# A 90-degree rotation of an 8192 x 8192 matrix: the first block of columns taken as 256, 256 and 512 rows and the last as 512 and 512, all loads in 16 KB rows, two of the last outputs in load buffers

## The chip, the cores and the metric

One core of a Trainium2 chip runs the kernel. The metric is the device time of one execution in microseconds (us). The kernel before takes 1276.25 us (median of three runs, 1274.88 to 1278.71). The limit for calling a kernel faster or slower is 2%.

## The reference

```python
x = np.random.randn(8192, 8192).astype(np.float32)   # 268 MB in, 268 MB out
def reference(x, k):        # k = 1
    return np.rot90(x, k)
```

Output row `8191 - c` is input column `c`. Nothing is computed: every element is read once and written once.

## The kernel before

The matrix is taken in blocks of 1024 rows by 4096 columns. A block is eight loads of 128 rows (2 MB each, 16 KB a row). VectorE copies each load into eight tiles `ar` of 512 columns, reversing the order of the columns inside each group of 128; TensorE transposes 128 x 128 pieces into PSUM, the memory that it writes to; ScalarE evicts (copies) PSUM into an output tile `ot` of 16 KB a partition (two evictions), and issues its transfer. A block has eight outputs of 2 MB.

```python
    a_pool = ctx.enter_context(tc.tile_pool(name="a_pool", bufs=2))   # loads
    r_pool = ctx.enter_context(tc.tile_pool(name="r_pool", bufs=68))
    o_pool = ctx.enter_context(tc.tile_pool(name="o_pool", bufs=2))   # outputs
    ...
def macro_tiles(N, M):
    for r0 in range(0, N, R):                     # R = 1024
        widths = [W] * (M // W)                   # W = 4096
        ...
        if r0 + R == N:
            widths[-1:] = [2048, 1024, 1024]
        ...
    for r0, c0, C in tiles:
        q = W // C                                # row groups of one load
        for t0 in range(0, RT, q):                # RT = 8
            if loads < 2:
                a = o_pool.tile([P, W], dt, tag="o")
            else:
                a = a_pool.tile([P, W], dt, tag="a")
            loads += 1
            nc.sync.dma_start(out=a, in_=x[...])  # queue of the SyncEngine
            ...                                   # eight VectorE copies a -> ar
        for g0 in range(0, C // P, G):            # G = 4
            ot = o_pool.tile([P, W], dt, tag="o")
            ...                                   # transposes, two evictions
                    nc.scalar.dma_start(out=dst, in_=o[...])   # queue of ScalarE
```

There are two buffers for loads and two for outputs, 16 KB a partition each, beside the 68 tiles `ar` of 2 KB. The first two loads borrow the output buffers, so four loads are queued at once. And a scheduler hands buffers to tiles and orders instructions; each engine then runs its own list in that order. In the views of the profile PE is TensorE, PEld its weight loads, DVE VectorE, ACT ScalarE, POOL GpSimd and SP the SyncEngine; a q after a name stands for the engine's sequencer, which issues transfers.

## Time and profile before

| | before |
|---|---|
| time | 1276.25 us |
| moved | 537.55 MB, mean 422 GB/s |
| busy: PE, ACT, DVE | 56%, 37%, 28% |
| first output issued | 54.4 us |
| last load landed | 1246.8 us |

From the profile's page, kernel before: the span, and then the mean busy share of the 16 DMA engines in tenths and the rate in GB/s, in 40 slices of 31.9 us.

```profile
span 1274.2 us, 10388 instructions
DMA  9999999999999999999999999999999999999998
GB/s 375 366 427 427 427 428 431 429 428 428 430 428 430 428 427 429 429 429 429 427 427 427 429 427 428 427 427 429 428 427 426 424 423 429 427 425 422 420 408 338
```

The kernel is bound by its transfers, and they are not at their best in the first two slices and the last two. The Trainium skill, "HBM Reference", section Specifications (TRN2), says that a core that streams alone reaches about 425 GB/s, bounded by its 16 DMA engines; the 427 to 431 of most middle slices agree within 2%. At 428 GB/s the bytes need 1256 us, so a change of the ends alone cannot win more than about 18 us, 1.4%.

The same kernel by windows. Columns: stretch in us, its length, busy time of PE, PEld, DVE, ACT and POOL with their instructions, granted clock of TensorE, busy share of the DMA engines, GB/s.

```profile
20.00:40.00 20.00, 2.06 (x6) 0.87 (x6) 8.97 (x26) 0.00 (x0) 0.00 (x0) 1.00 0.96 362
40.00:60.00 20.00, 11.94 (x78) 10.87 (x79) 8.32 (x24) 7.37 (x4) 0.00 (x0) 1.00 0.92 366
60.00:80.00 20.00, 7.17 (x40) 6.70 (x38) 5.55 (x16) 3.67 (x3) 0.00 (x0) 0.66 1.00 415
...
1240.00:1250.00 10.00, 5.50 (x41) 5.22 (x42) 2.77 (x8) 5.72 (x4) 0.00 (x0) 0.92 0.80 337
1250.00:1260.00 10.00, 8.04 (x63) 7.53 (x62) 0.00 (x0) 6.24 (x4) 0.00 (x0) 0.91 0.87 365
1260.00:1270.00 10.00, 3.05 (x28) 2.77 (x26) 0.00 (x0) 4.66 (x3) 0.00 (x0) 0.77 0.91 383
```

From 20 to 54 us the loads run alone in two buffers, because no output can start before eight loads have landed. From 80 to 160 us the rate is 427 to 433. At the end the last load lands at 1246.8 us, and from 1240 us on the transfers that are left move 337 to 383 GB/s.

### The profile page before, as it was taken

Reading aid. Unit: us, or ns where it says so; the run is one execution under the profiler, and the core shown is the slowest. Engines: PE = TensorE matmul, PEld = TensorE weight load, DVE = VectorE, ACT = ScalarE, POOL = GpSimd, SP = SyncE. Lnnn points to the kernel's source line nnn. Section 1 sums busy time; section 2 is a strip of 40 time slices with the busy share of each in tenths; the row PEclk is TensorE's granted clock in tenths of the full one; section 3 lists DMA queues with packets and bytes.
Section 4 is the critical chain, followed back from the end, with each engine's and each line's share of the span. In section 5 each row is a group of like instructions: output and inputs, shape, how many; then the busy total and the mean of one; then the engine's idle time right before and its main releaser. Section 6 shows DMA issues by size and latency. Waiting matters only on the chain.

```text
span 1274.2 us, 10388 instructions
## 1 busy us (share of the span) xinstructions
PE 719.2 (56%) x4096; PEld 685.5 (54%) x4096; DVE 355.2 (28%) x1024; ACT 466.9 (37%) x257; POOL 0.7 (0%) x6
## 2 busy tenths in 40 slices
PE   1455556556655665556546565565565665665564
PEld 0355556555554655556546555565555554665564
DVE  4422232223222322232223222322232222321210
ACT  0233343334334333343334333433343333434444
POOL 0000000000000000000000000000000000000000
PEclk9968686877777677776886867768777778678878
DMA  9999999999999999999999999999999999999998
GB/s 375 366 427 427 427 428 431 429 428 428 430 428 430 428 427 429 429 429 429 427 427 427 429 427 428 427 427 429 428 427 426 424 423 429 427 425 422 420 408 338
DMA packets 39105, 537.55 MB, mean 422 GB/s; under 512 B 4112, under 2 KB 4112, under 8 KB 6160
## 3 DMA queue, kind: packets, MB, share of 16 engines
q1 hardware_dynamic: 20480, 268.44, 49.8%
q10 hardware_dynamic: 18576, 268.44, 49.8%
q8 instruction: 32, 0.52, 0.2%
q14 instruction: 17, 0.14, 0.0%
HBM read 268.44 MB, written 268.44 MB: 421 GB/s over the span
## 4 chain that ended last, share of the span: by engine, by line
DMA 84%; DVE 12%; issue 2%; ACT 1%; PE 0%; DVEq 0%; SPq 0%; ACTq 0%
DMA a<-in_x_dram 81%; DVE ar L111 12%; DMA out_dram<-ot 3%; ACT ot L133 1%; PE ps L128 0%; DVEq L111 0%; SPq L100 0%; ACTq L133 0%; ACTq L141 0%
## 5 line engine op out<-in xcount | busy, mean ns | idle before, releaser
L128 PE MATMUL ps<-ident,ar 128*128 128x128 f32 x4096 | 719.2, 358 | 543.8 <-ACT ot L133 500.2
L128 PEld LDWEIGHTS ps<-ident,ar 128*128 128x128 f32 x4096 | 685.5, 192 | 577.3 <-ACT ot L133 530.5
L133 ACT COPY ot<-ps 128x2048 f32<-128x2048 f32 x256 | 465.6, 1870 | 789.3 <-DMA out_dram<-ot 733.5
L111 DVE COPY ar<-a 128x512 f32<-128x512 f32 x1024 | 355.2, 421 | 894.4 <-DMA a<-in_x_dram 894.4
L133 ACT ACT_TABLE_LOAD x1 | 1.3, 1283 | 10.9 <-DVE ar L111 10.9
masks.py:199 POOL TENSOR_SCALAR_AFFINE_SELECT ident<-ident 128x128 f32<-128x128 f32 x1 | 0.3, 292 | 0.1
masks.py:197 POOL MEMSET ident<- 128x128 f32 x1 | 0.2, 204 | 0.3 <-POOLq L160 0.3
L160 POOL MEMSET const-bfloat16-1.0<- 128x1 bf16 x1 | 0.1, 102 | 0.0
L160 POOL MEMSET const-uint8-127<- 128x1 uint8 x1 | 0.1, 102 | 0.0
L160 POOL MEMSET const-float32-0.0<- 128x1 f32 x1 | 0.1, 99 | 0.2 <-issue 0.2
L160 POOL MEMSET const-float32-1.0<- 128x1 f32 x1 | 0.1, 99 | 0.0
## 6 DMA issues: line engine op xcount, KB each, us to landing
a<-in_x_dram SPq DMA_DIRECT2D x128, 2048.0 KB, 16.6
out_dram<-ot ACTq DMA_DIRECT2D x127, 2048.0 KB, 15.9
out_dram<-ot ACTq DMA_DIRECT2D x2, 1024.0 KB, 5.7
```

Of the source, the lines that this page charges most:

```text
L111: nc.vector.tensor_copy(out=ar[:], in_=a[:, u, j * CH : (j + 1) * CH].rearrange("r (b m) -> r b m", m=P)[:, :, ::-1],)
L128: nc.tensor.transpose(ps[:, PW - 1 - w, t * P : (t + 1) * P], chunks[t, g * P // CH][:, g % (CH // P), :], ident,)
L133: nc.scalar.copy(o[:, G - PW - h : G - h, :], ps[:])
L160: nc = _bacc.Bacc("TRN2", target_bir_lowering=False, num_devices=1)
```

## The change

The intent: start the first outputs earlier by a first block that is complete after two loads, keep all loads at 16 KB a row at the end as well, and let the last block's first two outputs use the load buffers that have gone idle.

```diff
-        widths = [W] * (M // W)
-        if r0 + R == N:
-            widths[-1:] = [2048, 1024, 1024]
+            rows = [RT]
+            if r0 == 0 and c0 == 0:
+                rows = [2, 2, 4]
+            if r0 + RT * P == N and c0 + W == M:
+                rows = [4, 4]
...
-            if loads < 2:
-                a = o_pool.tile([P, W], dt, tag="o")
+            if loads in (2, 3):
+                a = o_pool.tile([P, E], dt, tag="o")
...
+        R = rt * P
+        G = E // R          # E = 4096: an output tile stays 16 KB a partition
...
-            ot = o_pool.tile([P, W], dt, tag="o")
+            if last and g0 < 2 * G:
+                ot = a_pool.tile([P, E], dt, tag="a")
+            else:
+                ot = o_pool.tile([P, E], dt, tag="o")
```

Output tiles keep their size, so a block of fewer rows is written in shorter rows: 1 KB for 256 rows, 2 KB for 512, 4 KB for 1024. Note which loads take the output buffers: 2 and 3, the loads of the second block, in place of 0 and 1.

More of the change, by code (lines that the diff above doesn't have):

```diff
@@ L10 @@
 P = 128
-R = 1024
-RT = R // P
+RT = 8
 W = 4096
 CH = 512
-G = 4
-PW = 2
+E = 4096
+PB = 2048
 def whole_reads(nc):
@@ L46, in macro_tiles @@
 def macro_tiles(N, M):
-    for r0 in range(0, N, R):
-        widths = [W] * (M // W)
-        if r0 == 0:
-            widths[:1] = [4096]
-        if r0 + R == N:
-            widths[-1:] = [2048, 1024, 1024]
-        c0 = 0
-        for C in widths:
-            yield r0, c0, C
-            c0 += C
+    for r0 in range(0, N, RT * P):
+        for c0 in range(0, M, W):
+            rows = [RT]
[3 more added lines that the diff above has]
+                rows = [4, 4]
+            r = r0
+            for n in rows:
+                yield r, n, c0
+                r += n * P
 @with_exitstack
@@ L87 @@
     loads = 0
-    for r0, c0, C in tiles:
-        last = (r0, c0, C) == tiles[-1]
-        q = W // C
+    for r0, rt, c0 in tiles:
+        last = (r0, rt, c0) == tiles[-1]
+        R = rt * P
+        G = E // R
+        PW = PB // R
         chunks = {}
-        for t0 in range(0, RT, q):
-            if loads < 2:
-                a = o_pool.tile([P, W], dt, tag="o")
+        for t in range(rt):
+            if loads in (2, 3):
+                a = o_pool.tile([P, E], dt, tag="o")
             else:
@@ L98 @@
             loads += 1
-            a = a.rearrange("r (q c) -> r q c", q=q)
             nc.sync.dma_start(
-                out=a,
-                in_=x[r0 + t0 * P : r0 + (t0 + q) * P, c0 : c0 + C].rearrange(
-                    "(q r) c -> r q c", q=q
-                ),
-            )
-            for u in range(q):
-                for j in range(C // CH):
-                    ar = r_pool.tile([P, CH // P, P], dt, tag="ar")
-                    nc.vector.tensor_copy(
-                        out=ar[:],
-                        in_=a[:, u, j * CH : (j + 1) * CH].rearrange(
-                            "r (b m) -> r b m", m=P
-                        )[:, :, ::-1],
-                    )
-                    chunks[t0 + u, j] = ar
-        for g0 in range(0, C // P, G):
-            ot = o_pool.tile([P, W], dt, tag="o")
+                out=a[:], in_=x[r0 + t * P : r0 + (t + 1) * P, c0 : c0 + W]
+            )
+            for j in range(W // CH):
+                ar = r_pool.tile([P, CH // P, P], dt, tag="ar")
+                nc.vector.tensor_copy(
+                    out=ar[:],
+                    in_=a[:, j * CH : (j + 1) * CH].rearrange(
+                        "r (b m) -> r b m", m=P
+                    )[:, :, ::-1],
+                )
+                chunks[t, j] = ar
+        for g0 in range(0, W // P, G):
+            if last and g0 < 2 * G:
+                ot = a_pool.tile([P, E], dt, tag="a")
+            else:
+                ot = o_pool.tile([P, E], dt, tag="o")
             o = ot.rearrange("m (g f) -> m g f", g=G)
-            S = PW if last and g0 + G == C // P else G
+            S = PW if last and g0 + G == W // P else G
             for h in range(0, G, PW):
@@ L126 @@
                     g = g0 + h + w
-                    for t in range(RT):
+                    for t in range(rt):
                         nc.tensor.transpose(
```

## The prediction

> **What bounds the kernel now.** The DMA engines. The page shows 537.55 MB in a 1274.2 us span, mean 422 GB/s, DMA tenths of 9 in all slices but the last; the middle slices hold 427 to 431 GB/s. PE is busy 56%, ACT 37%, DVE 28%. The Trainium skill, "DMA: Bandwidth & Descriptors", section Bandwidth, gives 435 GB/s as the ceiling of the SBUF ports and 425 GB/s for a 16 MB transfer; the middle of this trace agrees. The bytes don't change, so at 428 GB/s the kernel needs 537.55 MB / 428 GB/s = 1256 us. The change can win only the shortfall at the ends. From the view by windows, against 428 GB/s: 0 to 80 us moved 30.4 MB of 34.2, a loss of 8.9 us; from 1140 us on 53.5 MB of 57.4, a loss of 9.3 us. Some 5 us of the 18 (first latency, last eviction and receipt) stay whatever is done.
>
> **Fill.** Before, eight loads must land (47.9 us) ere the first output goes out (54.4 us). The first four are queued together and run at 426 GB/s; the next four have two buffers, each held by 2.77 us of DVE copies plus issue latency, so a pair takes 12.6 us in place of 9.8 (windows 20 to 50 us: 360, 363, 324 GB/s). After, two loads make a block: the first output is issued near 18 us (second landing 13.0, then two PSUM tiles, 1.87 us of eviction each). By the order view, the second block's two loads use output buffers, so they wait for the first two outputs to land (near 28 and 35 us), and the third block's first two loads are issued before them. The outputs fill that gap for DMA, then four loads run back to back. But blocks two and three bring six outputs beside the eight loads of the first whole block, so a stretch of loads alone moves to about 110 us, and costs one pair's 2.8 us. Outputs of 1 KB (8 MB) and 2 KB rows (8 MB) may run below the present 4 KB ones. Gain: about 2 us of the 8.9.
>
> **Drain.** Before, 8 KB and 4 KB load rows take 21 to 22 us in flight in place of 16.6, outputs overtake them, ACT stalls 7.1 us on a load near 1200 us, and the rate falls to 393-403, then 337-383 GB/s after 1240 us. After, loads keep 16 KB rows and end some 20 us earlier; about nine outputs follow alone. With two buffers a write-only pair costs 9.8 us plus an estimated 1.4 us (eviction and issue latency, partly hidden); the last block's four outputs have four buffers and run back to back. Gain: 4 to 5 us of 9.3, less 1 us if 2 KB rows write slower.
>
> **Middle.** Unchanged: 428 GB/s, same instruction counts.
>
> **Predicted time:** 1270 us, 8 in 10 between 1261 and 1278. Faster by over 2% (below 1251) is under the floor: 1%. Within 2%: 97%. Slower by over 2%: 2%.
>
> **What would show it.** First output issue near 18 us in place of 54; windows of 20 to 50 us at 400 GB/s or more; a dip near 100 to 125 us; last load landing near 1225 us, not 1247; windows from 1200 us at 400 or more but for the last 5 us; no ACT wait of 7 us on a load; middle slices 427 to 431.
>
> **What would make it wrong.** 1 KB rows writing at, say, 300 GB/s would cost 8 us. The loads that wait for outputs could leave DMA idle near 25 to 40 us. Writes alone could run well below 400 GB/s for the final 40 us. If all gaps close, 1261 us.

## The result

The changed kernel takes 1295.52 us (median of four runs, 1294.33 to 1297.01) against 1276.99 us for the kernel before in the same rounds. The ratio is 1.0146, with a 95% interval of 1.0127 to 1.0166. Ratios here and below are the mean time of one kernel's fast runs over that of the other's of the same rounds, so not quite the ratio of the medians that are quoted. By the 2% rule this is "the same", but it is clearly slower, by about 18.6 us (0.0146 x 1276.6).

From the page of the changed kernel (slices of 32.3 us):

```profile
span 1292.5 us, 10410 instructions
DMA  9799999999999999999999999999999999999988
GB/s 364 241 385 421 390 428 429 428 428 429 430 429 428 429 429 428 426 428 429 428 427 429 426 426 429 427 428 427 428 426 427 422 426 429 426 424 427 427 366 358
```

The middle is what it was. The second slice fell to 241 GB/s, and the third and the fifth are low too. By windows, changed kernel:

```profile
20.00:40.00 20.00, 3.50 (x31) 3.02 (x28) 0.00 (x0) 5.32 (x3) 0.00 (x0) 0.65 0.99 346
40.00:60.00 20.00, 9.67 (x54) 8.90 (x55) 10.92 (x32) 3.74 (x2) 0.00 (x0) 0.58 0.52 197
60.00:80.00 20.00, 6.04 (x33) 5.17 (x32) 5.55 (x16) 3.78 (x3) 0.00 (x0) 0.59 1.01 380
80.00:100.00 20.00, 11.06 (x77) 10.13 (x75) 5.55 (x16) 7.50 (x5) 0.00 (x0) 0.84 1.00 390
100.00:120.00 20.00, 6.54 (x36) 5.62 (x36) 5.55 (x16) 7.00 (x4) 0.00 (x0) 0.67 1.01 423
120.00:140.00 20.00, 2.92 (x10) 1.72 (x10) 7.52 (x22) 0.00 (x0) 0.00 (x0) 0.50 0.96 380
...
1240.00:1250.00 10.00, 8.18 (x66) 7.67 (x66) 0.56 (x2) 6.63 (x5) 0.00 (x0) 0.93 0.82 346
1250.00:1260.00 10.00, 7.70 (x56) 7.42 (x55) 0.00 (x0) 5.01 (x4) 0.00 (x0) 0.83 0.91 378
1260.00:1270.00 10.00, 7.92 (x69) 7.12 (x67) 0.00 (x0) 8.65 (x6) 0.00 (x0) 1.00 0.90 377
```

Summed over windows of 20 us from 0 to 160 us, the kernel before moved 64.8 MB and the changed kernel 57.5 MB; the 7.3 MB that are missing take 17 us at 428 GB/s. From 1200 us to its end the kernel before lost about 9 us against 428 GB/s and the changed one about 10. The loss lies in the start, and the gain of the end never came.

Between 48 and 56 us nearly nothing moved at all (windows of 2 us, changed kernel):

```profile
34.00:36.00 2.00, 0.00 (x0) 0.00 (x0) 0.00 (x0) 0.00 (x0) 0.00 (x0) 0.50 1.05 229
...
48.00:50.00 2.00, 0.00 (x0) 0.00 (x0) 0.23 (x1) 0.00 (x0) 0.00 (x0) 0.50 0.10 41
50.00:52.00 2.00, 0.99 (x5) 0.99 (x6) 1.47 (x5) 0.00 (x0) 0.00 (x0) 0.50 0.00 0
52.00:54.00 2.00, 2.00 (x11) 2.00 (x10) 2.00 (x7) 0.00 (x0) 0.00 (x0) 0.50 0.03 8
54.00:56.00 2.00, 2.00 (x12) 2.00 (x11) 2.00 (x7) 1.49 (x1) 0.00 (x0) 0.50 0.01 4
```

This hole is about 8 of the 17 us. The rest lies mostly in low rates: 229 to 360 GB/s from 32 to 40 us, when by the issue times below one load and one output were under way, and 380 to 390 from 60 to 100 us.

Why there is a hole, is told by VectorE's line of time and by the load issues, changed kernel. Columns: start, length, engine, line, operation, output and input, how many; in brackets the idle time before and what ended it.

```profile
12.94 2.77 DVE L109 COPY ar<-a 128x512 f32<-128x512 f32 x8 [2.12 <-DMA a<-in_x_dram]
...
45.46 2.77 DVE L109 COPY ar<-a 128x512 f32<-128x512 f32 x8 [29.74 <-DMA a<-in_x_dram]
...
50.53 8.14 DVE L109 COPY ar<-a 128x512 f32<-128x512 f32 x24 [2.30 <-DMA a<-in_x_dram]
```

```profile
10.85 0.33 SPq L102 DMA_DIRECT2D a<-in_x_dram  x1
15.74 0.33 SPq L102 DMA_DIRECT2D a<-in_x_dram  x1
31.51 0.33 SPq L102 DMA_DIRECT2D a<-in_x_dram  x1
41.22 0.33 SPq L102 DMA_DIRECT2D a<-in_x_dram  x1
56.02 3.01 SPq L102 DMA_DIRECT2D a<-in_x_dram  x2
```

The loads issued at 10.85 and 15.74 us belong to the third block; they took the two load buffers and landed at 19.4 and 25.4 us. The loads of the second block use output buffers, and could be issued only when the first two outputs had landed, at 31.51 and 41.22 us. The compiled program lists VectorE's copies in the order of the blocks (the first copy of each load, every eighth row; notes added at the right; the prediction's "order view" shows such lists):

```
## DVE, by row of its list
 1 ar_77 <-a_75     first block, load 0
 9 ar_95 <-a_93     first block, load 1
17 ar_189<-a_187    second block, in an output buffer (waits)
25 ar_207<-a_205    second block, in an output buffer (waits)
33 ar_301<-a_299    third block, issued before the two above
41 ar_319<-a_317    third block
```

So VectorE stood 29.7 us before the second block's first load. The third block's two loads kept both load buffers until 56 us, and in the end there was nothing left to transfer. The SyncEngine's own waits say the same: after the issue at 41.22 us it waited for VectorE, the longest such wait of the run. Columns: in total, times, longest in us.

```profile
SPq L102 <- DVE ar L109: 364.2, 124, 14.7
```

The run of 24 copies without a wait at 50.53 us is the second block's second load and the third block's two.

### The profile page after: what moved, and what is told of

Its sections match the earlier page's. It is cut to its first block, busy times and chain, and to the rows that moved or that the text cites. A ratio compares the mean times of both kernels' runs of the same rounds, so it can differ in the third digit from the quotient of the medians.

```text
span 1292.5 us, 10410 instructions
## 1 busy us (share of the span) xinstructions
PE 719.9 (56%) x4096; PEld 685.2 (53%) x4096; DVE 355.1 (27%) x1024; ACT 467.2 (36%) x257; POOL 0.7 (0%) x6
## 4 chain that ended last, share of the span: by engine, by line
DMA 78%; ACT 18%; DVE 1%; PE 1%; issue 1%; ACTq 0%; SPq 0%; DVEq 0%
DMA out_dram<-ot 70%; ACT ot L135 18%; DMA a<-in_x_dram 7%; DVE ar L109 1%; PE ps L130 1%; ACTq L143 0%; ACTq L135 0%; SPq L102 0%; DVEq L109 0%
## 6 DMA issues: line engine op xcount, KB each, us to landing
out_dram<-ot ACTq DMA_DIRECT2D x127, 2048.0 KB, 15.9
```

## The experiments

Times are medians of four runs unless said otherwise. "Before" in the same rounds was 1276.2 to 1276.6 us, so the last column, (ratio - 1) x 1276.6 us, is what compares runs of different rounds.

| run | what it is | us | ratio to before (95%) | us over before |
|---|---|---|---|---|
| changed | | 1295.52 | 1.0146 (1.0127-1.0166) | +18.6 |
| `start_only` | changed start, old end | 1291.03 | 1.0121 (1.0106-1.0136) | +15.4 |
| `end_only` | old start, changed end | 1277.60 | 1.0010 (0.9993-1.0026) | +1.3 |
| `no_o` | no load in an output buffer | 1287.18 | 1.0089 (1.0074-1.0104) | +11.4 |
| `o01` | loads 0, 1 in output buffers | 1282.66 | 1.0054 (1.0039-1.0069) | +6.9 |
| `third_first` | third block's loads and copies before the second's | 1285.69 | 1.0075 (1.0046-1.0104) | +9.6 |
| `rows4k` | changed, first outputs in 4 KB rows | 1285.64 | 1.0074 (1.0056-1.0092) | +9.4 |
| `o01_rows4k` | `o01`, first outputs in 4 KB rows | 1277.75 | 1.0006 (0.9991-1.0021) | +0.8 |
| `first44` | `o01`, first block 512 and 512 rows | 1278.09 | 1.0014 (0.9999-1.0029) | +1.8 |
| `end_no_a` | `end_only`, no output in a load buffer | 1277.41 | 1.0005 (0.9989-1.0022) | +0.6 |
| `fill4` | before, loads 4, 5 in output buffers too | 1272.34 | 0.9964 (0.9949-0.9979) | -4.6 |
| `fill4_end4` | `fill4` and a mended end | 1268.49 | 0.9937 (0.9917-0.9958) | -8.0 |
| `fill4_end8` | the same, last block whole | 1268.99 | 0.9944 (0.9927-0.9960) | -7.1 |
| `wr1k` | before, all outputs in 1 KB rows | 1473.43 (one run) | | +197 |
| `wr2k` | before, all outputs in 2 KB rows | 1286.25 (one run) | | +10 |

### start_only and end_only: which end of the kernel?

`start_only` is the changed kernel with the last block's columns, and the buffers of its outputs, as before (cut):

```diff
-            if r0 + RT * P == N and c0 + W == M:
-                rows = [4, 4]
+            cols = [W]
+            if r0 + RT * P == N and c0 + W == M:
+                cols = [2048, 1024, 1024]
```

> First block in 256, 256 and 512 rows with loads 2 and 3 in output buffers, as in the changed kernel; last block in columns as before. Theory W (the second block's loads wait for the first outputs to land, VectorE takes its copies in program order, so loads that have landed keep both load buffers and DMA runs dry) and rival R (the 1 KB and 2 KB output rows write slowly) both put the loss in the start: 1291 to 1296 us, and the windows of 48 to 56 us near 0 GB/s. Rival E (the new last block is what costs) says 1275 to 1279 us.

`end_only` is the changed kernel without the first block's edit:

```diff
-            if r0 == 0 and c0 == 0:
-                rows = [2, 2, 4]
-            if loads in (2, 3):
+            if loads in (0, 1):
```

> First block as before (one block of 1024 rows, loads 0 and 1 in output buffers), last block in 512 and 512 rows as in the changed kernel. W and R: 1276 to 1280 us, since by the windows against 428 GB/s the end lost 10.3 us after the change and 9.3 before it. E: 1288 us or more.

Measured: 1291.03 and 1277.60 us. The start costs 15 us, the end nothing that stands clear of the spread. Theory E falls. The hole is in `start_only` too, a little earlier: 0 to 98 GB/s from 46 to 54 us.

### no_o and o01: which loads may wait for an output?

```diff
-            if loads in (2, 3):
+            if loads in ():          # no_o
+            if loads in (0, 1):      # o01
```

> The changed kernel, but every load takes a load buffer, none an output buffer: no load waits for an output. W says that most of the 17 us lost in the start come back: 1276 to 1284 us, VectorE's first long wait for a load well under the present 29.7 us, and no window near 0 GB/s. R says that the rows are as short as before and the time stays at 1290 us or more.

> The changed kernel, but loads 0 and 1 take the output buffers, as in the kernel before, instead of loads 2 and 3; four loads are queued at once and nothing waits for an output to land. W: 1272 to 1280 us, a few us under the run without output buffers. R: 1290 us or more.

Measured: 1287.18 and 1282.66 us. Both lie between what W and R expected. Taking the waiting loads away gives back 7.2 us of the 18.6; queueing four loads at once instead of two gives another 4.5. VectorE's longest wait in `no_o` is 10.5 us in place of 29.7, and no stretch is near 0 GB/s. But 6.9 us remain with `o01`, so W is only a part; the rest may be the short rows (R2) or loads that run alone (L).

### o01_rows4k and first44: what remains?

`o01_rows4k` writes the first block's eight outputs, tiles unchanged, to the places of the first eight outputs of the kernel before. The values are wrong; bytes, tiles, waits and order stay.

```diff
+                    if r0 < RT * P and c0 == 0:
+                        top = M - (wide + 1) * 512
+                        wide += 1
+                        nc.scalar.dma_start(
+                            out=out[top : top + 512, 0:1024].rearrange("(g m) f -> m g f", g=4),
+                            in_=ot.rearrange("m (g f) -> m g f", g=4),
+                        )
+                        continue
```

> The run o01 (1282.7 us), but the eight outputs of the first block are written in 4 KB rows to the places where the kernel before writes its first eight: same tiles, waits, bytes and order, wrong values on purpose. Theory R2 (what is left of the loss in the start is the short output rows: while 1 KB rows are written, 24 to 72 us, both queues together move 370 to 400 GB/s and some engines trail) says 1277 to 1279 us, with 415 GB/s or more in that stretch. Rival L (what is left is the loads that run alone at 72 to 84 and 124 to 142 us, as too few outputs lie beside them) says 1281 to 1283 us.

`first44`:

```diff
-                rows = [2, 2, 4]
+                rows = [4, 4]        # and loads 0, 1 in output buffers
```

> The run o01 with the first block in 512 and 512 rows in place of 256, 256 and 512: no 1 KB rows, only one stage where loads run alone. R2: 1277 to 1279 us (2 KB packets took 624 ns against 611). L: 1278 to 1281 us.

Measured: 1277.75 and 1278.09 us, within R2's range for both; L's range for the first is missed. `first44` lies in L's range as well, so it doesn't decide. The windows of `o01` and then of `o01_rows4k` show it where 1 KB rows are written:

```profile
36.00:46.00 10.00, 5.93 (x32) 5.69 (x32) 2.77 (x8) 3.63 (x2) 0.00 (x0) 0.61 1.03 380
46.00:56.00 10.00, 0.69 (x2) 0.29 (x2) 2.77 (x8) 3.63 (x2) 0.00 (x0) 0.56 1.01 378
```

```profile
36.00:46.00 10.00, 5.67 (x27) 5.67 (x28) 2.99 (x9) 3.63 (x2) 0.00 (x0) 0.50 1.01 431
46.00:56.00 10.00, 1.99 (x10) 1.06 (x8) 2.82 (x9) 3.63 (x2) 0.00 (x0) 0.67 1.01 430
```

The DMA engines are busy all the time in both; with 1 KB rows they move 12% less. With the waits mended and the rows long, nothing is left of the loss: +0.8 us, as `end_only` has +1.3. The early outputs, for which the first block was cut up, win nothing either: with 4 KB rows and four queued loads the kernel is level with the one before. The stretch of loads alone has only moved: in `o01_rows4k` the windows from 100 to 140 us fall to 397 and 392 GB/s.

### third_first: the wait itself, or VectorE's order?

```diff
+    first, second, third = tiles[:3]
+    store(*first, load(*first), 0, 2, "oo")
+    c_third = load(*third)          # its loads and copies stand first,
+    c_second = load(*second)        # these still take output buffers and wait
+    store(*second, c_second, 0, 2, "oo")
+    store(*third, c_third, 0, 4, "oooo")
```

> The changed kernel with one thing moved: the four loads of the third block and their VectorE copies stand before the two loads of the second block, which still take the output buffers and still wait for the first two outputs to land. Theory W-order (VectorE's program order is what runs DMA dry: landed loads of the third block wait behind the second block's) says no window near 0 GB/s and 1283 to 1289 us, near the 1287.2 of no_o. Rival W-slot (the wait for the outputs' landing itself is the loss) says 1292 to 1296 us.

Measured: 1285.69 us, the middle of two pairs of runs (1282.9 and 1283.0; 1288.4 and 1288.8), both within W-order's range. Why they differ is open; the profile is of a slower one. No window of 2 us between 44 and 56 us is below 287 GB/s. VectorE's line of time in this run:

```profile
18.74 2.77 DVE L104 COPY ar<-a 128x512 f32<-128x512 f32 x8 [3.06 <-DMA a<-in_x_dram]
...
25.23 2.77 DVE L104 COPY ar<-a 128x512 f32<-128x512 f32 x8 [3.71 <-DMA a<-in_x_dram]
```

The third block's first two loads landed at 18.7 and 25.2 us and were copied at once. In the changed kernel the same two loads were issued at the same place, and their copies began after 50.5 us. The second block's loads still wait for outputs to land, and yet 9.0 of the 18.6 us are back. The order of the lists made the wait expensive; W-order holds and W-slot falls. The move changed two lists, however: in the SyncEngine's, too, the third block's last two loads now stand before the waiting ones (issued at 21.5 and 28.0 us). This run doesn't separate the two. That the hole itself was VectorE's doing is read from the SyncEngine's wait of 14.7 us for VectorE in the changed kernel.

### rows4k: do the two costs add?

The edit of `o01_rows4k`, made to the changed kernel itself.

> The changed kernel, its first eight outputs written in 4 KB rows to the places of the kernel before; wrong values on purpose, nothing else changed. If the cost of short rows adds to that of the wait, 1289 to 1292 us (4 to 6 us less than the changed kernel, and the gap near 50 us stays). If it is hidden behind the wait, 1293 to 1296 us.

Measured: 1285.64 us, 9.2 us less than the changed kernel, outside both ranges. The gap is still there, but it comes sooner: the second block's loads are issued at 30.2 and 36.2 us in place of 31.5 and 41.2, and the third block's next two at 51.3 in place of 56.0. A waiting load pays for the short rows of the output that it waits for. On the mended order the rows are worth 6.1 us (`o01` to `o01_rows4k`), on the order of the change 9.2. The issue times suggest that the costs do not simply add; by the intervals of the table, some 3 us on each figure, the two sizes are not clear of each other.

### wr1k and wr2k: the length of the output rows by itself

The kernel before, with each output tile written as 16 rows of 1 KB (or 8 of 2 KB) a partition; places permuted. Their outputs are wrong, which doesn't matter for the times. The last output also goes out in one transfer in place of two (cut).

```diff
-                    top = M - c0 - (g0 + done) * P
-                    dst = out[top : top + S * P, r0 : r0 + R].rearrange("(g m) f -> m g f", g=S)
+                    n, part = divmod(outs, 4)
+                    top = (n % 4) * 2048
+                    left = n // 4 * R + part * 256
+                    dst = out[top : top + 2048, left : left + 256].rearrange("(g m) f -> m g f", g=16)
```

> The kernel before with every output of the whole matrix written in 1 KB rows (places permuted, wrong values on purpose): the cost of the row length by itself. If 1 KB rows hold both queues to about 380 GB/s, as in the stretch of 24 to 72 us of o01, 1380 to 1440 us. If that stretch was slow for another reason, under 1300 us.

> As wr1k (1473 us), with 2 KB rows for every output. If the cost goes by the number of rows, it is less than half of the 197 us that 1 KB rows added: 1350 to 1375 us. If only rows of 1 KB are slow, as the packets of 622 to 625 ns in the 2 KB stage of the changed kernel suggest (611 with 4 KB rows), 1280 to 1300 us.

Measured, one run each: 1473.43 and 1286.25 us. The page of `wr1k`: rate in 40 slices, and the outputs from issue to landing (15.9 us in the kernel before).

```profile
GB/s 369 374 371 370 366 365 365 374 370 372 372 371 361 371 367 371 372 359 368 369 368 370 366 372 369 366 374 374 366 366 367 374 369 368 368 363 352 345 333 305
...
out_dram<-ot ACTq DMA_DIRECT2D x128, 2048.0 KB, 19.0
```

1 KB rows hold the whole kernel to about 369 GB/s, and its time is above the expected range; 2 KB rows cost about 10 us in 537 MB. The cost does not go by the number of rows. Spread over 128 outputs, 1 KB rows cost 197 / 128 = 1.54 us an output and 2 KB rows 10 / 128 = 0.08. The changed start writes four outputs of each: an estimate of 6.5 us, beside the 6.1 us found by taking the short rows away. That both row lengths step by the same 32 KB from row to row is a property of the matrix; whether the length alone or the length with this step is slow was not separated.

`wr2k` shows one thing more. Its loads and their buffers are those of the kernel before, and yet its eighth load landed at 43.4 us and its windows of 20 to 40 us moved 414 GB/s; the other four profiles with that start (`before`, `end_only`, `end_no_a`, `wr1k`) have 47.1 to 48.5 us and 354 to 362 GB/s. Why is open. Had this start gone as the others, the cost of 2 KB rows would be an estimated 4 to 5 us larger (the difference of these landings), which is still little beside 197.

### end_no_a: what do the idle load buffers bring?

```diff
-            if last and g0 < 2 * G:
-                ot = a_pool.tile([P, E], dt, tag="a")
-            else:
-                ot = o_pool.tile([P, E], dt, tag="o")
+            ot = o_pool.tile([P, E], dt, tag="o")
```

> The run end_only (1277.6 us) with the last block's outputs in the two output buffers alone. If the idle load buffers keep the last outputs back to back, taking them away costs 2 to 4 us: 1279.5 to 1281.5 us, and the issues of the last four outputs are 5.5 to 6 us apart in place of 4.3. If the eviction and the transfer set the pace anyhow, 1277 to 1278.5 us.

Measured: 1277.41 us, no slower than `end_only`. The issues of the last outputs do draw apart, from 4.3 us to 5.0 to 5.6, but it decides nothing. The likely reason is in the windows of `end_only`:

```profile
1220.00:1230.00 10.00, 6.86 (x49) 6.38 (x48) 2.77 (x8) 6.81 (x4) 0.00 (x0) 0.83 0.61 257
1230.00:1240.00 10.00, 6.39 (x57) 5.84 (x56) 0.00 (x0) 6.19 (x5) 0.00 (x0) 1.00 0.99 415
1240.00:1250.00 10.00, 8.94 (x64) 8.42 (x63) 0.00 (x0) 6.74 (x4) 0.00 (x0) 0.83 0.76 321
```

The last load lands at 1220.9 us. At that moment outputs are issued about 10 us apart (1206.05, 1215.89, then 1225.14), the pace at which they shared the engines with loads, so when the loads end the engines run short at once (257 GB/s). The load buffers are given to outputs of the last block, five or more outputs later, when the gap has passed.

### fill4, fill4_end4 and fill4_end8: mending both ends

`fill4` is the kernel before with one edit. The output buffers lie idle until the first output; loads 4 and 5 may use them as well.

```diff
-            if loads < 2:
+            if loads in (0, 1, 4, 5):
```

> The kernel before with one edit: loads 4 and 5 also take the output buffers, which lie idle until the first output at 50 us, so the eight loads of the first block cycle through four buffers. If the two load buffers are what limits the start of the kernel before (a pair in 12.6 us in place of 9.8), the eighth load lands near 43 us in place of 47.9 and the time is 1270 to 1273 us. If something else limits loads that run alone, 1275 to 1277 us.

Measured: 1272.34 us. The eighth load lands at 43.0 us in place of 47.9. The window of 20 to 40 us rises from 362 to 431 GB/s:

```profile
20.00:40.00 20.00, 2.76 (x8) 1.16 (x8) 10.76 (x32) 1.28 (x1) 0.00 (x0) 1.00 1.01 431
```

The other two kernels with this edit, below, have 43.0 us and 430 to 431 GB/s as well. That two load buffers always hold the start back is not shown, since `wr2k` ran almost as fast with two.

`fill4_end4` adds a new end. The loads of the last two half blocks are allotted before the last output of the block ahead, and outputs then take turns through four buffers:

```diff
+    store(*full, c_full, 0, 7, "ooooooo")
+    c_half = load(*half)            # 512 rows
+    c_rest = load(*rest)            # 512 rows
+    store(*full, c_full, 7, 8, "a") # the buffer of the last load but one
+    store(*half, c_half, 0, 4, "ooaa")
+    store(*rest, c_rest, 0, 4, "ooaa", last=True)
```

> A version meant to beat both: fill4, and a last block in 512 and 512 rows whose outputs take turns through four buffers, the last output of the block before it going first into the load buffer that the second to last load leaves. If the gap near 1240 us and the two-buffer pace of 5.7 us an output after it are the loss of the end, 1263 to 1267 us. If writes alone are limited by something else, 1270 us or more.

`fill4_end8` keeps the last block whole (`store(*rest, c_rest, 0, 8, "ooaaooaa", last=True)`), so all outputs have 4 KB rows.

> fill4_end4 (1268.5 us) with the last block whole: 1024 rows, every output in 4 KB rows, the same four buffers in turn. Its first output needs the last load, about 3 us after it landed, where the split block needs only its fourth load; against that, 16 MB go out in 4 KB rows in place of 2 KB. If the split is what keeps the end fed, 1270 to 1273 us; if the buffers do that, 1266 to 1269 us.

Measured: 1268.49 and 1268.99 us, the first a little above the range of its theory, between the two ranges given for it; the second inside the range that says that the buffers decide and not the split. The windows of `fill4_end4`, where the last load lands at 1217.2 us:

```profile
1210.00:1220.00 10.00, 9.22 (x71) 8.70 (x71) 2.84 (x9) 7.38 (x4) 0.00 (x0) 0.89 1.00 425
1220.00:1230.00 10.00, 7.86 (x70) 7.30 (x69) 0.00 (x0) 7.63 (x5) 0.00 (x0) 1.00 1.00 418
1230.00:1240.00 10.00, 8.46 (x74) 7.67 (x71) 0.00 (x0) 8.65 (x5) 0.00 (x0) 1.00 1.01 421
```

The gap after the last load is gone, and outputs alone run at 416 to 421 GB/s from 1220 to 1260 us (411 to 431 in `fill4_end8`, after one window at 378 when its loads end). Both versions beat the kernel before by about 0.6%, with intervals clear of 1, though "the same" by the 2% rule; the difference between them is within the spread. Over `fill4` the new end brings 3.4 and 2.5 us, but the intervals overlap. It changes the order of the loads, the buffers of the outputs and the length of the load rows together, and which of them closes the gap is not shown.

## Why the prediction was wrong

It forecast a gain of some 6 us and the kernel lost 18.6; 1295.5 us lies well above its 1261 to 1278. That the class "within 2%" came out is luck: neither end did what it was given for.

**What bounds the kernel, and the middle: right.** The middle slices hold 422 to 430 GB/s after the change, and the floor near 1256 us was not touched by any run.

**Fill, "four loads run back to back": wrong, and this is the step that failed first.** The prediction saw in the order view that the second block's loads wait for outputs and that the third block's loads are issued before them, but this is the SyncEngine's list. It let the outputs "fill that gap for DMA" and the four loads follow, and says nothing of VectorE's list, where the second block's copies stand before the third's. The loads issued early could therefore not give their buffers back. Measured: VectorE idle for 29.7 us, nearly no transfer from 48 to 56 us (0 to 41 GB/s), and windows of 20 to 50 us at 285 to 390 GB/s where 400 or more was forecast. Moving the third block's loads and copies ahead (`third_first`) brought back 9.0 us and taking the waiting loads away (`no_o`) 7.2.

**Fill, loads queued at the start: overlooked.** The change also gave up the four loads that were queued at once. `no_o` against `o01` prices that at 4.5 us.

**Fill, "outputs of 1 KB ... may run below": right in kind, mis-sized.** The sum held the start's gain at 2 us with little for the rows. They cost 6.1 us with the order mended and 9.2 without, and 1.54 us an output by `wr1k`. The prediction named 8 us as a thing that could make it wrong; neither this nor the size in the sum came from the trace, since no 1 KB row was in it.

**Fill, landings and the first output: late.** First output at 21.7 us against 18 predicted, landings at 31.5 and 41.2 against 28 and 35. For the first output it counted the evictions only; 6.4 us of transposes lie on the chain before the second one. The rest is in part the short rows: with long ones the landings came at 30.2 and 36.2 (`rows4k`). The stretch of loads alone came at 120 to 140 us (380 GB/s), as described, a little later.

**Drain, "gain 4 to 5 us": wrong.** The part on the load rows held: while loads last, the windows from 1200 to 1230 us move 421 to 430 GB/s where the kernel before had 393 to 403, and ScalarE's wait of 7.1 us for a load is gone. The last load did land earlier against the end: 54.7 us before the end (1237.8 of 1292.5), where before it was 27.4 (1246.8 of 1274.2). But earlier loads only made the stretch of outputs alone longer, and that stretch ran at 346 to 400 GB/s. The prediction priced the two-buffer pace well (two pairs of issues lie 10.6 and 11.1 us apart, 11.2 were forecast) and left out the gap when the loads end. In the changed kernel it is here:

```profile
1236.00:1238.00 2.00, 0.00 (x0) 0.00 (x0) 0.22 (x1) 1.47 (x1) 0.00 (x0) 0.97 0.87 369
1238.00:1240.00 2.00, 1.55 (x8) 1.56 (x9) 2.00 (x7) 2.00 (x2) 0.00 (x0) 0.50 0.23 98
1240.00:1242.00 2.00, 2.00 (x14) 2.00 (x14) 0.56 (x2) 0.16 (x1) 0.00 (x0) 0.67 0.37 156
```

`end_only` measured +1.3 us, within the spread. The use of load buffers by the first two of the last block's four outputs, credited with back-to-back writes, was worth nothing that could be measured (`end_no_a`).

**The sum.** From the changed kernel by steps: waiting loads 7.2 us, loads not queued 4.5, short rows 6.1, and 0.8 left; together 18.6 over the kernel before. By the intervals of the table each step is uncertain by about 3 us. The steps were taken in this order; in another order the rows come to 9.2, as said above.

## What to carry to other kernels

Before letting one load borrow another tile's buffer, read the instruction lists of every engine that has to consume the loads, not only the list that issues them: in the changed kernel one late load in VectorE's list held two landed loads behind it for over 30 us. In a kernel bound by transfers, cutting blocks to start sooner shortens the rows that are written, so price the row length by a run first. Lending idle buffers to loads at the start won 4.6 us here (`fill4`), and together with a new order and new buffers at the end 7.1 us with every output still in 4 KB rows (`fill4_end8`).

## What the Trainium skill lacked or had wrong

- "DMA: Bandwidth & Descriptors", section Specifications, gives 512 B as the smallest transfer for line rate. Here outputs in 1 KB rows held the kernel to a mean of 365 GB/s (1473 us), where 4 KB rows had 422 GB/s (1276 us) and 2 KB rows 419 (1286 us). Writes to HBM in rows of 1 KB, 32 KB apart, are well above 512 B and not at line rate; the page has no table by row length for HBM writes on this chip. Elsewhere the skill warns of small transfers and times a single 1 KiB descriptor, but no page has such a table. That the rows and not their step of 32 KB are slow was not separated here.
- The same page, section Rules for kernel authors, asks for at least 1 MiB a transfer for the most bandwidth. The size alone does not settle the rate: loads of 2 MB alone on one queue moved 354 to 362 GB/s in two buffers in four profiles (20 to 40 us; but 414 in `wr2k`) and 431 in four buffers (`fill4`). No page tells how many transfers must be queued.
